# A hybrid attention and mLSTM decoder trunk in float32: the mLSTM's gates, running maximum and what goes with them placed at the end of attention instead of between its first units

## The chip, the cores and the metric

The kernel runs on one core of one Trainium2 chip. A core has a matrix engine (TensorE, here PE, with its weight loads as PEld), a vector engine (VectorE, DVE), a scalar engine (ScalarE, ACT), a general engine (GpSimd, POOL) and a queue engine (SyncE, SP) that issues DMAs. Each engine runs its own list of instructions in order and waits on semaphores for the others. Matrix products are written to PSUM, which is divided into banks of 128 x 512 float32.

The metric is the device time of one execution in microseconds, as the median of several runs.

## The reference

Two layers over 512 tokens of width 1024. Each layer computes, after an RMS norm:

```python
z = h @ w_in      # q_a | k_a | v_a | q_m | k_m | v_m | o_m | i/f gate logits | gates A, B
att = sliding_window_attention(q_a, k_a, v_a, sinks)        # 8 heads of 64, 2 kv heads, window 128
i_pre, f_pre = jnp.split(if_m + m_gate_bias, 2, axis=-1)
hm = mlstm_chunkwise(q_m, k_m, v_m, i_pre, f_pre)           # 4 heads, qk 64, v 128
mixed = sigmoid(g_a) * (att @ w_att_branch) + sigmoid(g_m) * (rmsnorm(hm) * sigmoid(o_m) @ w_m_branch)
x = x + mixed @ w_out
x = x + relu(rmsnorm(x) @ w_ff1)**2 @ w_ff2
```

The part that the change moves is the scalar side of the mLSTM: from the gate logits of 4 heads,

```python
log_f = log_sigmoid(f_pre);  b = cumsum(log_f)              # decay up to each token
m_t = max(b + m_prev, max over s <= t of (b_t - b_s + log_i_s))   # running maximum, the stabiliser
w   = exp(b_t - b_s + log_i_s - m_t) * (q_t . k_s)          # weights of the mLSTM
h   = (w @ v + ...) / max(|den|, exp(-m_t))
```

## The kernel before

All products keep float32 accuracy by splitting each operand into a high and a low part: a weight tile `w` of 128 x 512 is loaded by SP, ACT copies its rounded part to `wh` (L197) and DVE subtracts to get `wl` (L198). A projection is a group of four output banks (named mm in the profile) over eight chunks of 128 input rows; a chunk takes 4 x 3 = 12 matmuls of 512 columns.

In `mixer` a helper, `weave`, walks through a list of such steps, the fill, each of which counts 0.25, and calls side steps at given positions of that count (one unit is one chunk of 12 matmuls). After it a scheduler orders the instructions of each engine by what it expects to be ready, so an instruction does not stand exactly where the position says, but the positions set who comes first among what is ready. The fill here is: the mLSTM's q and k (positions 0 to 8), two groups of gate A (8 to 24), the mLSTM's v (24 to 32), the attention branch (32 to 40), a group of gate B (40 to 48), the o gate (48 to 56) and the last gate group.

The side steps are, in this order:

- Attention, in eight units: four blocks of 128 queries by two key/value heads. Of each unit: `att_scores` twice (product with kT, then ACT L567 or a memset and DVE's predicated copy L568 out of PSUM), `att_softmax` (maximum L575, L576, L578; four exponentials L581 and one L583; division L584 to L586), `att_probs` (four transposes, split by ACT L207 and DVE L208, masks on POOL L600 and L602), `att_out` (products with v2, then ACT L614, DVE L618, ACT L621, DVE L622). For each block, `k_tr` and `q_tr` transpose keys and queries (ACT L526, L527, L548; DVE L528, L529, L549). Unit i has its first score product at position 7 + 1.65 i and its `att_out` 5.65 later.
- `gating0`: i and f gates, log sigmoid (L405 to L417; twelve small operations on DVE and ACT).
- `gating1`: six small products with `lf` give sums along the tokens into an aux bank; DVE copies them to `bl` and `gr` (L426, L427), forms `acol` (L428) and the ten entries of `bias` (L431, L433).
- `gating2`: four transposes of `acol` into one aux bank, then four scans on DVE (L445), one a block, each started from the block before through `mp` (L448).
- `gating3`: the running maximum `cm` is split to `cm2` by ACT (L463) and DVE (L464), four small transposes of it and DVE's L468 and ACT's L470 give `em`.
- `qk_split` splits the mLSTM's q and k (L642 to L650).
- `m_decay` (product of `sel` with `cm2`, copied by ACT L710), `m_weights` (DVE L717, ACT L718 and L721, POOL L723, a product of k and q, DVE L729) and `m_out` (products with `vm`, then L737 to L742), for four heads from position 28 on.

All side steps share the PSUM pool aux, which has three banks here; a step's first product waits for a bank, which is free again when its last reader is done. ACT changes its function table between exponentials and the sigmoids of the gates (L655; `back` restores the table, L661).

Of the kernel before, what the change touches and what calls it, by code (L numbers as in the profile page):

```python
# [33 lines left out]
def hybrid_kernel(ctx, tc, x, norm_mix, w_in, att_q_norm, att_k_norm, att_sinks, m_gate_bias,  # L34
# [324 lines left out]
    def mixer(l, norm, late, order, phase):  # L359
# [154 lines left out]
        def k_vec(b):  # L514
            rope(kvi[:, b, 0:128].rearrange("p (h d) -> p h d", d=HD), b, HKV)

        def k_tr(b):

            ps = aux([P, P])
            pe.transpose(ps, kvi[:, b, 0:128], ident)  # L520
            for h in range(HKV):
                r = slice(64 * h, 64 * h + 64)
                o = slice(64 - 64 * h, 128 - 64 * h)
                c = slice((b + 1) * P, (b + 2) * P)
                g = gcols[1][r, l:l + 1]
                sc.activation(kTh[r, h, c], ps[r, :], AF.Copy, scale=g)  # L526
                sc.activation(kTh[o, h, c], ps[r, :], AF.Copy, scale=g)  # L527
                ve.scalar_tensor_tensor(kTl[r, h, c], ps[r, :], g, f32(kTh[r, h, c]), op0=ALU.mult, op1=ALU.subtract)  # L528
                ve.tensor_copy(kTl[o, h, c], f32(kTl[r, h, c]))  # L529

        def q_vec(b):
            rope(q_tok[b].rearrange("p (h d) -> p h d", d=HD), b, HQ)

        def q_tr(b):


            ps = aux()
            for j in range(4):
                pe.transpose(ps[:, j * P:(j + 1) * P], q_tok[b][:, j * P:(j + 1) * P], ident)
            for j in range(2):  # L540
                qT[b, j] = temp(F32R)
                t4 = qT[b, j].rearrange("p (n i t) -> p n i t", n=2, i=2)
                p4 = ps[:, 2 * j * P:2 * (j + 1) * P].rearrange("p (n t) -> p n t", n=2)
                for i in range(2):
                    r = slice(64 * i, 64 * i + 64)
                    o = slice(64 - 64 * i, 128 - 64 * i)
                    g = gcols[0][r, l:l + 1]
                    sc.activation(t4[r, :, i, :], p4[r], AF.Copy, scale=g)  # L548
                    ve.scalar_tensor_tensor(t4[o, :, i, :], p4[r], g, f32(t4[r, :, i, :]), op0=ALU.mult,  # L549
                                            op1=ALU.subtract)  # L550
# [87 lines left out]
        def qk_split(m, i):  # L638
            t = qk_raw[m]
            r, o = slice(64 * i, 64 * i + 64), slice(64 - 64 * i, 128 - 64 * i)  # L640
            d = slot(F32R)
            sc.activation(d[r], t[r], AF.Copy)  # L642
            if m < 2:
                gp.tensor_copy(d[o], f32(d[r]))
                low = slot(F32R)
                gp.memset(f32(low[o]), 0.0)
                ve.tensor_tensor(low[r], t[r], f32(d[r]), op=ALU.subtract)
                m_q[2 * m + i], m_ql[2 * m + i] = d, low
            else:
                ve.tensor_tensor(d[o], t[r], f32(d[r]), op=ALU.subtract)  # L650
                m_k[2 * (m - 2) + i] = d
# [24 lines left out]
        def ev_v(b, ps):  # L676
            if b == 0:
# [6 lines left out]
        side = [(0, lambda: k_vec(0)), (0, lambda: q_vec(0)), (0, lambda: k_vec(1)), (0, lambda: q_vec(1)),  # L684
                (7 - 1.25, lambda: k_tr(0)), (7 - 1.75, lambda: q_tr(0))]
        for i, (b, kv) in enumerate(units):
# [6 lines left out]
            if kv == 0 and b + 1 < NB:  # L693
                if b + 2 < NB:
                    side += [(at + 1, lambda b=b: k_vec(b + 2)), (at + 1, lambda b=b: q_vec(b + 2))]
                side += [(at + 2 * 1.65 - 1.25, lambda b=b: k_tr(b + 1)), (at + 2 * 1.65 - 1.75, lambda b=b: q_tr(b + 1))]
        side += [(8.45 + 3.0 * i, f) for i, f in enumerate((gating0, gating1, gating2, gating3))]
        side += [(9.6 + 1.65 * n, lambda n=n: qk_split(n // 2, n % 2)) for n in range(8)]
        g0, s0 = gate_steps(0)
        g1, s1 = gate_steps(1, lambda: back(sigmoid(g0 + g1)))  # L700
# [579 lines left out]
    for l in range(DEPTH):  # L1280
        with start if l == 0 else ExitStack() as phase:
            if l > 0:
                psum_pools(phase, 3)
            norm = mixer(l, norm, late, order, phase)
        late = norm.steps(1, 1.5, 0.5)
        with ExitStack() as phase:
            psum_pools(phase, 2)
            norm = mlp(l, norm, late, phase)
        late = norm.steps(0, 1.5, 0.5, lambda k, norm=norm: turn_behind(norm, k)) if norm else []
        order = [4, 5, 6, 7, 0, 1, 2, 3]  # L1290
# [40 lines left out]
```

## Time and profile before

| | us |
|---|---|
| median of 3 runs | 1310.16 |
| lowest and highest run | 1309.24, 1310.36 |
| the profiled execution | 1309.12 |
| its span | 1307.4 |
| TensorE busy in it | 1288.9 |
| VectorE, ScalarE, GpSimd busy | 954.2, 762.6, 219.3 |

The span goes from the first to the last instruction of the profiled execution. The granted clock was 1.00 throughout. In the views below, a row of the order of time gives start, length, engine, line, operation, output and inputs with sizes and a count; in brackets stands how long the engine was idle before and what ended that. A group's row gives busy us and the mean of one in ns.

The busy time of 40 slices, in tenths, shows the two layers, each with its attention and mLSTM first and its feed-forward part behind:

```profile
PE   8999999999999999999999999999999999999998
PEld 6877788888889999999888777888888899999986
DVE  4689754465677897968957896545737879879797
ACT  5468755444465665656554787554445556665563
POOL 4513300000003021131115223000000030301210
```

Counted from 1, attention of layer 0 is in slices 3 to 5 and that of layer 1 in slices 22 to 25 (32.7 us each): there VectorE is at its busiest outside the feed-forward part, and ScalarE at its busiest of all.

### The profile page before, as it was taken

To read this page: it belongs to the slowest core of one execution; us is meant where nothing else is said; L and a number is where in the kernel's file an instruction comes from. 1 tells how busy PE (TensorE), PEld (TensorE's weight loads), DVE (VectorE), ACT (ScalarE), POOL (GpSimd) and SP (SyncE) were. 2 spreads that over 40 slices of the span, in tenths; PEclk is the share of its full clock that TensorE was granted. 3 is DMA by queue.
4 is the path that set the end of the run, shared out by engine and by line. 5 is a ranking of instruction groups with operands and counts; after the bars stand their busy time and mean duration, and the time that the engine had idled before them with its cause. 6 is when DMAs were issued, how large, how long until landed. Compare 5 with 4: busy or idle time off the path is not lost.

```text
span 1307.4 us, 19100 instructions
## 1 busy us (share of the span) xinstructions
PE 1288.9 (99%) x6966; PEld 1103.1 (84%) x6966; DVE 954.2 (73%) x1501; ACT 762.6 (58%) x1327; POOL 219.3 (17%) x303
## 2 busy tenths in 40 slices
PE   8999999999999999999999999999999999999998
PEld 6877788888889999999888777888888899999986
DVE  4689754465677897968957896545737879879797
ACT  5468755444465665656554787554445556665563
POOL 4513300000003021131115223000000030301210
PEclk9999999999999999999999999999999999999999
DMA  5322222372369888897124222223714597988953
GB/s 154 110 73 65 65 76 78 89 243 87 97 154 171 237 185 206 197 209 213 33 70 117 65 65 73 76 79 90 256 56 129 143 214 193 204 212 196 213 144 95
DMA packets 129855, 177.62 MB, mean 136 GB/s; under 512 B 9816, under 2 KB 77504, under 8 KB 129760
## 3 DMA queue, kind: packets, MB, share of 16 engines
q1 hardware_dynamic: 93664, 131.69, 33.4%
q0 software_dynamic: 35520, 44.17, 21.2%
q8 instruction: 55, 0.90, 0.3%
q10 hardware_dynamic: 576, 0.53, 0.1%
q14 instruction: 40, 0.33, 0.1%
HBM read 174.27 MB, written 2.10 MB: 135 GB/s over the span
## 4 chain that ended last, share of the span: by engine, by line
PE 91%; DVE 4%; ACT 2%; issue 1%; POOL 1%; DMA 1%; DVEq 0%; ACTq 0%; POOLq 0%; SPq 0%
PE mm L47 74%; PE aux L47 15%; PE aux L52 2%; DVE wl L198 1%; ACT wh L197 1%; ACT t L581 0%; DMA w<-in_w_in_dram 0%; POOL t L602 0%; DVE t L618 0%; POOL t L476 0%; DVE t L208 0%; DMA grow<-in_norm_mix_dram 0%; DVE a L650 0%; DVE t L568 0%; DVE m L575 0%
## 5 line engine op out<-in xcount | busy, mean ns | idle before, releaser
L47 PE MATMUL mm<-i,wh 128*128 128x512 f32 (+1 forms) x1280 | 353.1, 362 | 0.3 <-ACT kvi L381 0.3
L836 ACT ACTIVATE wh<-raw 128x1024 fp32r<-128x1024 f32 x212 | 223.0, 1055 | 181.6 <-PE mm L47 110.7
L837 DVE TENSOR_TENSOR wl<-raw,wh 128x1024 fp32r<-128x1024 f32 x212 | 255.3, 1218 | 74.7 <-ACT wh L836 74.4
L47 PEld LDWEIGHTS mm<-i,wh 128*128 128x128 f32 x1280 | 223.8, 189 | 32.8 <-DVE a L668 0.9
L198 DVE TENSOR_TENSOR wl<-w,wh 128x512 fp32r<-128x512 f32 (+1 forms) x208 | 141.1, 682 | 131.3 <-ACT wh L197 122.7
L47 PE MATMUL mm<-i,wl 128*128 128x512 f32 (+1 forms) x640 | 230.4, 360 | 0.0
L197 ACT ACTIVATE wh<-w 128x512 fp32r<-128x512 f32 (+1 forms) x208 | 127.1, 612 | 139.9 <-PE mm L47 102.6
L47 PE MATMUL mm<-wh,uh 128*128 128x512 f32 x448 | 174.9, 390 | 0.0
L47 PE MATMUL mm<-wl,uh 128*128 128x512 f32 x448 | 174.8, 390 | 0.0
L47 PE MATMUL mm<-wh,ul 128*128 128x512 f32 x448 | 174.3, 389 | 0.0
L991 POOL DMA_DIRECT2D raw<-in_w_ff_dram x48 | 62.5, 1309 | 594.0 <-DVE i L211 284.3
L47 PE MATMUL mm<-wh,i 128*128 128x512 f32 (+1 forms) x512 | 150.0, 370 | 0.4 <-ACT wh L197 0.4
L47 PEld LDWEIGHTS mm<-i,wl 128*128 128x128 f32 x640 | 121.0, 189 | 18.4 <-DVE wl L837 0.4
L47 PEld LDWEIGHTS mm<-wh,i 128*128 128x128 f32 x512 | 92.1, 189 | 16.2 <-ACT wh L197 0.8
L879 DVE SCALAR_TENSOR_TENSOR x<-mm,ms,x 128x512 f32<-128x512 f32 x128 | 91.9, 744 | 12.2 <-PE mm L47 12.2
L47 PEld LDWEIGHTS mm<-wh,ul 128*128 128x128 f32 x448 | 84.1, 188 | 17.7
L47 PEld LDWEIGHTS mm<-wh,uh 128*128 128x128 f32 x448 | 84.3, 188 | 16.3
L47 PEld LDWEIGHTS mm<-wl,uh 128*128 128x128 f32 x448 | 84.3, 188 | 16.0
L47 PE MATMUL mm<-wl,i 128*128 128x512 f32 (+1 forms) x256 | 93.4, 365 | 0.0
L47 PE MATMUL mm<-wh,a 128*128 128x512 f32 x256 | 81.3, 393 | 0.0
L47 PE MATMUL mm<-a,wh 128*128 128x512 f32 x256 | 80.5, 397 | 0.0
L47 PE MATMUL aux<-t,wh 128*128 128x256 f32 x384 | 69.5, 283 | 0.0
(247 smaller groups left out, 2157.6 us busy)
## 6 DMA issues: line engine op xcount, KB each, us to landing
raw<-in_w_ff_dram SPq DMA_DIRECT2D x144, 512.0 KB, 5.2
raw<-in_w_ff_dram POOLq DMA_DIRECT2D x84, 512.0 KB, 7.9
w<-in_w_in_dram SPq DMA_DIRECT2D x128, 256.0 KB, 2.7
w<-in_w_out_dram SPq DMA_DIRECT2D x32, 256.0 KB, 2.9
w<-in_w_att_branch_dram SPq DMA_DIRECT2D x16, 256.0 KB, 2.7
w<-in_w_m_branch_dram SPq DMA_DIRECT2D x16, 256.0 KB, 2.8
w<-in_w_in_dram SPq DMA_DIRECT2D x16, 128.0 KB, 2.1
out_dram<-x SPq DMA_DIRECT2D x8, 256.0 KB, 2.0
```

The costliest lines, as they stand in the source:

```text
L47: latest[0] = nc.tensor.matmul(*args, **kw)
L52: return nc.tensor.transpose(*args)
L197: sc.activation(wh[:, :off], raw[:, :off], AF.Copy)
L198: ve.tensor_tensor(wl[:, :off], raw[:, :off], f32(wh[:, :off]), op=ALU.subtract)
L836: sc.activation(hi, src, AF.Copy)
L837: ve.tensor_tensor(lo, src, f32(hi), op=ALU.subtract)
L879: ve.scalar_tensor_tensor(xh, ps[:, i, :], ms[j][:, b:b + 1], xh, op0=ALU.mult, op1=ALU.add)
L991: gp.dma_start(to[h], src(h, i, j), accum_op=ALU.add)
```

## The change

One line of `mixer` gives the positions of the four gating steps. They were 8.45, 11.45, 14.45 and 17.45, between the score products of the first and the last units of attention; they become 20.5, 22.25, 24.0 and 25.75, around the probabilities and outputs of the last units and shortly before `m_decay` at 28. No operation is added, removed or resized.

```diff
-        side += [(8.45 + 3.0 * i, f) for i, f in enumerate((gating0, gating1, gating2, gating3))]
+        side += [(20.5 + 1.75 * i, f) for i, f in enumerate((gating0, gating1, gating2, gating3))]
```

The side steps that stand beside it in the code:

```python
units = [(b, kv) for b in range(NB) for kv in range(HKV)]
...
    at = 7 + 1.65 * i
...
side += [(9.6 + 1.65 * n, lambda n=n: qk_split(n // 2, n % 2)) for n in range(8)]
...
    at = 28 + 4.65 * h
    side.append((at, lambda h=h: m_decay(h)))
```

## The prediction

> **What bounds the kernel now.** I read the page first, then the busy time by stretch for the two attention stages, then what TensorE waited for there, then the order of time around those waits.
>
> ```profile
> PE 1288.9 (99%) x6966; PEld 1103.1 (84%) x6966; DVE 954.2 (73%) x1501; ACT 762.6 (58%) x1327; POOL 219.3 (17%) x303
> ...
> PE 91%; DVE 4%; ACT 2%; issue 1%; POOL 1%; DMA 1%; DVEq 0%; ACTq 0%; POOLq 0%; SPq 0%
> ```
>
> TensorE is busy 1288.9 of 1307.4 us and is 91% of the chain that ended last. The change takes no matmul away and adds none, so it can only alter TensorE's idle time. How much of that lies where the change acts is in the next view, with layer 0 in the first four rows and layer 1, 646.9 us later, in the last three.
>
> ```profile
> 62.00:104.40 42.40, 41.07 (x216) 32.68 (x215) 37.05 (x97) 30.45 (x89) 13.83 (x29) 1.00 0.26 69
> 104.40:150.00 45.60, 44.04 (x210) 34.24 (x209) 40.39 (x93) 38.52 (x96) 13.37 (x20) 1.00 0.25 67
> 150.00:161.50 11.50, 11.03 (x50) 8.54 (x50) 7.83 (x20) 7.65 (x22) 3.51 (x7) 1.00 0.21 61
> 161.50:200.00 38.50, 38.50 (x196) 32.70 (x195) 21.76 (x62) 21.96 (x62) 2.63 (x8) 1.00 0.30 82
> ...
> 708.90:751.30 42.40, 40.99 (x216) 32.63 (x215) 37.18 (x97) 30.34 (x89) 13.45 (x28) 1.00 0.26 69
> 751.30:796.90 45.60, 44.10 (x210) 34.21 (x209) 40.43 (x92) 38.53 (x96) 13.41 (x20) 1.00 0.25 67
> 796.90:808.40 11.50, 11.03 (x50) 8.54 (x50) 7.85 (x20) 7.66 (x22) 3.51 (x7) 1.00 0.19 59
> ```
>
> The columns are length, then the busy time of PE, PEld, DVE, ACT and POOL, the granted clock, and DMA. Attention of one layer shows 1.33 + 1.56 + 0.47 = 3.4 us of idle TensorE, and the mLSTM behind it none. DVE is busy 37.05 of 42.40 and 40.39 of 45.60 us (87% and 89%) in attention, ACT 72% and 84%; after it both fall under 60%. So attention is where VectorE and ScalarE sometimes make TensorE wait, and the change moves VectorE work out of it into its last few microseconds. Both layers show the same rows, so I work on layer 0 and double.
>
> ```profile
> PE aux L47 <- POOL t L602: 0.9, 2, 0.5
> PE aux L47 <- DVE t L568: 0.8, 1, 0.8
> PE aux L47 <- DVE kT L528: 0.5, 1, 0.5
> PE aux L52 <- DVE t L445: 0.3, 1, 0.3
> PE aux L47 <- DVE m L576: 0.2, 1, 0.2
> PE aux L52 <- DVE t L549: 0.2, 1, 0.2
> ```
>
> These are TensorE's named waits from 62 to 161.5 us: 2.9 us. One of them, 0.3 us for L445, is for the moved work itself: a PSUM bank of the pool aux (three banks) that the four scans of the running maximum hold from their transposes until the last scan. The largest, 0.8 us for L568, is in the first units, ahead of everything that moves, and stays.
>
> **What a wait costs.** The idle shown is less than the time lost, as the pace shows.
>
> ```profile
> 261.55 54.62 PE mm L47 x240
> ```
>
> ```profile
> 113.49 0.39 PE L47 MATMUL mm<-i,wl 128*128 128x512 f32 x1
> 114.15 0.33 PE L52 MATMUL aux<-ident,t 128*128 128x128 f32 x1 [0.28 <-DVE t L445]
> ...
> 123.30 0.61 PE L47 MATMUL mm<-i,wh 128*128 128x512 f32 x2
> 124.43 0.36 PE L47 MATMUL aux<-kT,t 128*128 128x256 f32 x1 [0.52 <-DVE kT L528]
> ...
> 152.26 0.39 PE L47 MATMUL mm<-wl,i 128*128 128x512 f32 x1
> 153.01 0.50 PE L47 MATMUL aux<-t,v 128*128 128x512 f32 x1 [0.36 <-POOL t L602]
> 153.35 0.39 PE L47 MATMUL aux<-cm,sel 128*128 128x512 f32 x1
> ```
>
> Undisturbed, one matmul of 512 columns starts every 54.62/240 = 0.23 us. From 113.49 to 114.15 are 0.66 us, so 0.43 is lost where 0.28 is shown; a wait costs its shown idle plus about 0.15. In this measure the wait for L528 costs 123.30 to 124.43 less two matmuls, 1.13 - 0.46 = 0.67; and 2.9 shown is about 2.9 + 8 x 0.15 = 4.1 us a layer.
>
> **The change, part by part.** gating0 does not move: its operations are ready early, and in the new order it stands on DVE and ACT where it stood. gating1, gating2 and gating3 do move, in both layers alike. SP's queue issues the same loads in the same order, and POOL's queue changes one place; no DMA is added. ACT keeps its four table loads in attention at the same steps. In the new program order on TensorE gating1's six products stand right behind the transposes of the last attention unit's probabilities, the transposes of acol half a chunk of projection later, and the four small transposes of the running maximum one by one among the next chunk and a half; then comes the first product with sel, 2.25 chunks behind gating1. From the second weight product of the mLSTM on, both orders are equal.
>
> The moved instructions and their neighbours, from the groups by line and shape of 62 to 160 us:
>
> ```profile
> L618 DVE TENSOR_TENSOR t<-aux,t 64x256 f32<-64x256 f32 x16 | 6.6, 414 | 1.8 <-ACT t L614 1.5
> ...
> L622 DVE TENSOR_TENSOR a<-t,a 128x128 fp32r<-128x128 f32 x16 | 4.4, 297 | 0.4 <-ACT a L621 0.4
> ...
> L445 DVE TENSOR_TENSOR_SCAN t<-aux,mp,neg 4x128 f32<-4x128 f32 x4 | 1.9, 466 | 0.0
> ...
> L464 DVE TENSOR_TENSOR cm<-t,cm 4x512 fp32r<-4x512 f32 x1 | 0.7, 681 | 0.0
> ...
> L463 ACT ACTIVATE cm<-t 4x512 fp32r<-4x512 f32 x1 | 0.6, 633 | 0.0
> ...
> L448 DVE TENSOR_TENSOR mp<-t,gr 4x1 f32<-4x1 f32 x3 | 0.4, 142 | 0.0
> ...
> L426 DVE COPY bl<-aux 128x32 f32<-128x32 f32 x1 | 0.2, 179 | 0.0
> L428 DVE TENSOR_TENSOR acol<-ig,bl 128x16 f32<-128x16 f32 x1 | 0.2, 175 | 0.0
> ```
>
> ```profile
> 84.45 0.18 DVE L426 COPY bl<-aux 128x32 f32<-128x32 f32 x1
> ...
> 85.66 0.69 DVE L586 TENSOR_TENSOR t<-t,den 128x512 f32<-128x512 f32 x1
> 86.27 0.16 DVE L431 COPY bias<-acol 128x4 f32<-128x4 f32 x1
> ```
>
> *What attention gets back.* gating1's thirteen DVE operations ran from 84.45 to 86.43; with the softmax's L586 of 0.69 us between them taken off, they are some 1.2 us of DVE (busy times of neighbours overlap). The four scans are 1.9, the three L448 0.4, L464 0.7. So 4.2 us a layer leave DVE's queue in attention, 5% of its 77 us there, and one PSUM bank is free from acol's transposes to the last scan.
> - The wait for L445 goes: -0.43. Bounds: 0 (another holder of a bank takes its place) to -0.43.
> - The wait at 124.43 is for the last unit's keys. In the new order ACT runs all four L526/L527 for them without the L614 that stood between, so the second L528 comes sooner; I take -0.45, between 0 and -0.67.
> - The wait for L576 (0.2 shown, 0.35 lost) goes, but the probabilities of the fifth unit and the scores of the last now come in one cluster with it and need three banks at once: +0.2 net, between -0.35 and +0.6.
> - Of the two waits for L602 (0.9 shown, 1.2 lost), the later, 0.5, falls away because gating1 and acol now stand between the last probabilities and the products that need their masks; of the earlier I take 0.2 off. -0.7, between 0 and -1.2.
> - TensorE's own 1.1 us of gating leaves the early units and comes back at the end. TensorE then comes sooner to the keys of the third block and the second scores of the fifth unit, which wait for DVE: I take nothing as won or lost, bounds -0.3 (acol's own wait) and +0.5.
>
> Sum: -0.43 - 0.45 + 0.2 - 0.7 = -1.4 us a layer.
>
> *What the end of attention pays.* Here the whole chain gating1, gating2, gating3 has to be over before sel. DVE runs in order, and in the new order between L426 and L464 stand four L618, four L622, one weight split and em's sum: 4 x 0.41 + 4 x 0.25 + 0.7 + 0.2 = 3.5 us, beside 1.2 + 1.9 + 0.4 + 0.7 = 4.2 of the chain itself. With ACT's 0.6 for L463 and about 0.8 for the crossings to TensorE and back, sel is ready 9.1 us after gating1's products. TensorE's cover up to sel is 2.25 x 12 x 0.23 = 6.2 us of projection, 8 x 0.23 = 1.8 of attention output, and some 0.65 for the transposes of acol and of the running maximum: 8.7 us. Missing: 0.4 us a layer. Bounds: 0, since the L618 run while TensorE transposes acol, and 3.4 when the masks hold DVE up (second rival). Behind the waiting sel stand the first weight products and the projection's matmuls, and nothing else is in a hurry:
>
> ```profile
> 156.45 0.60 ACT L710 ACTIVATE t<-aux 128x512 f32<-128x512 f32 x1
> ```
>
> ```profile
> 167.11 0.38 PE L47 MATMUL aux<-vm,t 128*128 128x129 f32 x2
> ```
>
> The copy of sel's product, L710, ran 3 us after sel (153.35), and the first product that needs the weights made of it came 10.7 us after that. The weight splits that DVE delays by 0.6 us are made up to three chunks (8 us) ahead.
>
> Net: -1.4 + 0.4 = -1.0 us a layer, -2.0 us in all. The profiled execution took 1309.12 us (span 1307.40 and 1.72 around it); -2.0 makes 1307.1. The median of the runs shown lies 1.04 above the profiled one, so the forecast for it is 1308.2 us.
>
> **The rivals.** *The end is covered and attention flows better.* If nothing is missing before sel and the freed DVE time also removes the fifth unit's cluster wait and the rest of L528 and L602, a layer gains 0.43 + 0.67 + 0.35 + 0.9 = 2.35: 1310.16 - 4.7 = 1305.5. For it speaks that DVE is at 89%; against it that the first units' waits do not depend on what moves.
>
> *Slower: the masks hold the chain.* The moved sums with two SBUF inputs (L428, L433, L448) now fall beside POOL's masks of the last unit.
>
> ```profile
> 100.77 0.56 DVE L578 TENSOR_TENSOR es<-sinks,m 128x4 f32<-128x4 f32 x1
> ```
>
> ```profile
> 99.59 1.73 POOL L644 CAST a<-a 64x512 fp32r<-64x512 f32 x1 [25.72 <-ACT a L642]
> ```
>
> ```profile
> L602 POOL TENSOR_SCALAR_AFFINE_SELECT t<-t 128x512 fp32r<-128x512 f32 x12 | 9.5, 788 | 4.8 <-DVE es L578 2.5 <-DVE t L208 1.9
> ...
> L600 POOL TENSOR_SCALAR_AFFINE_SELECT t<-t 128x512 fp32r<-128x512 f32 x12 | 8.5, 712 | 20.4 <-ACT t L207 20.4
> ```
>
> L578, of four elements a partition, took 0.56 us and ended with POOL's cast at 101.3. The last unit has two L600 and two L602, 2 x 0.71 + 2 x 0.79 = 3.0 us. If DVE stands through all of them, sel misses 0.4 + 3.0 = 3.4 us a layer, and the layer loses 3.4 - 1.4 = 2.0: 1310.16 + 4.0 = 1314.2. It decides from 1.4 us missing on. Against it: L650 and L622, also with two SBUF inputs, ran at their usual length beside masks. The Trainium skill, SBUF — State Buffer, section Who interferes with whom, says that a DVE instruction with two SBUF inputs contends with a GpSimd instruction that reads SBUF and the second fully blocks. The row of L578 agrees; by the rule alone each such sum would wait for a mask's end, which is this rival's 1314.2.
>
> *Nothing is won.* The scheduler reorders some 400 matmuls, and each wait removed is followed by one like it at the next bank: 1310.2. For it speaks that the first score waits stay and that TensorE, arriving sooner, meets the same VectorE.
>
> **How the numbers follow.** Forecast 0.42, covered end 0.20, slower 0.25, nothing won 0.13. A measurement of this kernel can tell about 0.2%, 2.6 us, from no change. The forecast's 2.0 us gain is close to that: of its 0.42 I give 0.22 to faster, 0.19 to within, 0.01 to slower. So faster 0.22 + 0.20 = 0.42, within 0.19 + 0.13 = 0.32, slower 0.25 + 0.01 = 0.26. The forecast's own range, from its terms' bounds with not all at one end, is -2.2 to +0.3 us a layer: 1305.8 to 1310.8. The range for 8 in 10 reaches on to both rivals: 1303.5 to 1315.0.
>
> **What would show it.** Right: no wait of PE for L445 inside attention; TensorE's idle in the stretch that holds units three to seven falls below 1.56 us; a wait of 0.2 to 0.8 us in front of aux<-cm,sel or of the small transposes, released by L464 or L445. The covered end: no such wait at all. The masks: L428 and L433 of 0.5 us and more beside L600 and L602, and a wait over 1.4 us before sel. Nothing won: the same 3.4 us of idle a layer under other names. The forecast is wrong in its ground if the mLSTM behind, without idle now, shows waits for L729 or L680.

## The result, and the profile after

The changed kernel took 1311.70 us (median of 22 runs, 1310.85 to 1313.08) and the kernel before, on the same chip, 1310.26 (22 runs, 1308.73 to 1311.04). The ratio is 1.0014, with a 95% interval of 1.0008 to 1.0020: slower by 0.14%, 1.4 us by the medians and 1.8 by the ratio. That is less than the 0.2% that the prediction took as the least a measurement of this kernel can tell, but the interval doesn't reach 1, and the time has moved to the other side of the 2 us gain that was forecast. The profiled execution took 1311.39 us, its span is 1309.7.

TensorE's busy time on the page of the changed kernel is 1288.8 us (98%), what it was (1288.9 before), so the 2.3 us of span are idle or slower starts on TensorE. To place them I use three marks that both kernels have on TensorE: A, the transposes of the first block's queries; B, the transposes of the last unit's probabilities; C, the second weight product of the mLSTM, behind which both orders are equal. From A to C the same 309 matmuls of the projections stand in both kernels, 276 of them ahead of B. The place of A itself differs from profile to profile (61.03 and 61.44 here, 62.79 in the last run below, an edit of the kernel before that changes nothing up to there), so I compare distances between the marks and not spans. The rows of the order of time of the kernel before:

```profile
61.03 0.27 PE L52 MATMUL aux<-ident,a 128*128 128x128 f32 x1
...
149.97 0.40 PE L52 MATMUL aux<-ident,t 128*128 128x128 f32 x2
...
161.49 0.33 PE L47 MATMUL aux<-a,a 128*128 128x384 f32 x1
```

and of the changed kernel:

```profile
61.44 0.38 PE L52 MATMUL aux<-ident,a 128*128 128x128 f32 x2
...
149.16 0.30 PE L52 MATMUL aux<-ident,t 128*128 128x128 f32 x1 [0.17 <-ACT wh L197]
...
162.91 0.33 PE L47 MATMUL aux<-a,a 128*128 128x384 f32 x1
```

A to B went from 88.94 to 87.72 us, 1.2 less, since the TensorE work of gating1 to gating3 no longer stands there; B to C went from 11.52 to 13.75, 2.2 more. A layer pays 1.0 us. Layer 1 gives the same to 0.1 us (A to B 88.99 and 87.70, B to C 11.52 and 13.74).

What TensorE waited for, from 62 to 162.9 us (total, times, longest), in the changed kernel:

```profile
PE aux L52 <- DVE t L568: 1.3, 2, 0.8
PE aux L47 <- DVE t L568: 0.9, 1, 0.9
PE aux L47 <- DVE t L618: 0.8, 1, 0.8
PE aux L47 <- DVE kT L528: 0.7, 1, 0.7
PE aux L52 <- ACT a L621: 0.3, 1, 0.3
...
```

Beside the same view of before: the waits for L445, L576 and L549 are gone, and that for L602 (0.9) has left the list. New are 0.8 and 0.5 for L568 in front of the keys of the third and fourth block, and 0.8 for L618 in front of the first scores of the sixth unit; the 0.3 put down to L621 stand in front of the first small transpose, where the first scan had ended only 0.15 us before. The wait for L528, of which the forecast hoped to be rid, grew from 0.5 to 0.7. Why a removed delay came back as a wait is seen at the third block's keys. TensorE before:

```profile
93.25 0.61 PE L47 MATMUL mm<-i,wh 128*128 128x512 f32 x2
94.05 0.30 PE L52 MATMUL aux<-ident,kvi 128*128 128x128 f32 x1 [0.18 <-DVE t L549]
```

TensorE after:

```profile
92.58 0.39 PE L47 MATMUL mm<-i,wh 128*128 128x512 f32 x1
93.75 0.30 PE L52 MATMUL aux<-ident,kvi 128*128 128x128 f32 x1 [0.78 <-DVE t L568]
```

VectorE after:

```profile
91.04 0.69 DVE L198 TENSOR_TENSOR wl<-w,wh 128x512 fp32r<-128x512 f32 x1 [1.32 <-ACT wh L197]
...
93.17 0.44 DVE L568 COPY_PREDICATED t<-tri_l,aux 128x256 f32<-128x256 int32 x1
```

Counted from A, the keys' transpose starts 33.02 us behind it before and 32.31 after, so 0.7 is won. But TensorE was ready for it 1.3 us sooner (0.18 and 0.78 of idle time are to be taken off these starts); the other 0.6 became a longer wait. VectorE had stood idle for 1.32 us shortly before, waiting for ScalarE, so it wasn't short of time here: L568 came when its turn in the order came.

At the wait for L528 it was another thing. The second L528 of the last block started at 123.90, 0.44 sooner than before when counted from A, as the forecast had it, but TensorE was there 0.58 sooner. ScalarE's copy for it was over at 123.11, in the kernel before at 123.32 with L528 at 123.93: in both kernels VectorE came last, and the L614 that the forecast saw leave ScalarE's way was not what held it. Between the two L528 of the changed kernel stand L650 with 0.92 us and L529 with 0.65, which took 0.69 and 0.22 elsewhere.

At the end stands what the forecast had no price for. TensorE in the changed kernel, around the third and fourth of gating3's small transposes:

```profile
157.81 0.40 PE L47 MATMUL mm<-wh,i 128*128 128x512 f32 x1
158.14 0.22 PE L52 MATMUL aux<-ident,t 4*128 4x4 f32 x1
158.29 0.50 PE L47 MATMUL mm<-wh,i 128*128 128x512 f32 x1
158.63 0.39 PE L47 MATMUL mm<-wl,i 128*128 128x512 f32 x1
...
159.42 0.22 PE L52 MATMUL aux<-ident,t 4*128 4x4 f32 x1
...
160.84 0.40 PE L47 MATMUL aux<-cm,sel 128*128 128x512 f32 x1
```

From 157.81 to 158.63 stand two projection matmuls, 0.46 us at the undisturbed pace of 0.23, and one transpose of four columns: 0.82, so the transpose costs 0.36 us with no wait shown on PE. It starts 0.10 late, the matmul behind it 0.15 later, and the one behind that again 0.11 late. The product with sel, which the forecast saw waiting, starts right after its forerunner with no wait in brackets.

### The profile page after: what moved, and what is told of

The parts are those of the page before. It is cut to its first block, busy times and chain, and to the rows that moved or that the text cites. A ratio compares the mean times of both kernels' runs of the same rounds, so it can differ in the third digit from the quotient of the medians.

```text
span 1309.7 us, 19099 instructions
## 1 busy us (share of the span) xinstructions
PE 1288.8 (98%) x6966; PEld 1104.8 (84%) x6966; DVE 957.2 (73%) x1501; ACT 761.4 (58%) x1327; POOL 215.0 (16%) x303
## 4 chain that ended last, share of the span: by engine, by line
PE 93%; DVE 4%; ACT 1%; issue 1%; POOL 0%; DMA 0%; DVEq 0%; ACTq 0%; POOLq 0%
PE mm L47 76%; PE aux L47 14%; PE aux L52 2%; DVE wl L198 1%; ACT wh L197 1%; DVE t L618 0%; DVE t L208 0%; DVE t L549 0%; ACT t L581 0%; DVE a L650 0%; DMA grow<-in_norm_mix_dram 0%; DVE t L568 0%; DVE kT L528 0%; POOL t L602 0%; DVE kT L529 0%
## 5 line engine op out<-in xcount | busy, mean ns | idle before, releaser
L47 PE MATMUL aux<-i,wh 128*128 128x256 f32 x384 | 69.5, 283 | 0.0
```

Source lines behind the costliest of these rows:

```text
L47: latest[0] = nc.tensor.matmul(*args, **kw)
```

## Experiments

The theory with which I went in (A) was that the end got dearer because each of the four small transposes stands alone. Its rivals were that VectorE's chain is late there (B), and that the loss lies in the new waits of attention (C). All ratios are against runs of the kernel before on the same chip; line numbers of an edited kernel are shifted by the lines added (L570 or L577 for L568, for instance).

**The four together, in the changed kernel.**

```diff
-            for b in range(NB):
-                pe.transpose(cps[:, b * MH:(b + 1) * MH], cm[:, b * P:(b + 1) * P], ident[:MH, :MH])
+            last = pe.transpose(cps[:, 3 * MH:], cm[:, 3 * P:], ident[:MH, :MH])
+            with tc.issue_after(last.ins):
+                for b in range(NB - 1):
+                    pe.transpose(cps[:, b * MH:(b + 1) * MH], cm[:, b * P:(b + 1) * P], ident[:MH, :MH])
```

> The changed kernel, but the last gating step's four transposes of the running maximum to columns (128x4) stand together on TensorE instead of one by one between projection products; nothing else moves. Theory A (the end of attention got dearer because each of the four stands alone and costs about 0.36 us instead of 0.08): 0.7 to 1.0 us less in each layer, so 1.4 to 2.0 us under the changed kernel, about 1310 us. Theory B (the end got dearer because VectorE's chain of gating is late there, and TensorE waits for it): within 0.5 us of the changed kernel, the wait only moves from the first transpose to the group. Theory C (the loss is not at the end but in the new waits for aux banks between the units): within 0.3 us of the changed kernel.

Measured: 1310.09 us, ratio 1.0002 (0.9993 to 1.0011), level with the kernel before. A to B is 87.67 us as in the changed kernel, B to C 12.96 in place of 13.75. TensorE there:

```profile
157.75 0.61 PE L47 MATMUL mm<-wh,i 128*128 128x512 f32 x2
158.87 0.38 PE L52 MATMUL aux<-ident,t 4*128 4x4 f32 x4 [0.51 <-DVE t L445]
...
159.52 0.63 PE L47 MATMUL mm<-wh,i 128*128 128x512 f32 x2
```

The group has to wait for the last scan, 0.51 us, which the four apart did not, and is cheaper all the same: 1.77 us from 157.75 to 159.52 less three matmuls (two ahead of the group, one behind it), 0.69, is 1.08 with the wait, against 1.77 for the four apart (0.69, the first of them with a wait of 0.31, then 0.36, 0.36 and 0.35). As A expected (1.6 us under the changed kernel); B's lateness exists, with 0.5 us, but is not what made the kernel slower.

**One by one and together, in the kernel before.** A function `small_tr(b)` issues one transpose behind the latest matmul, `gating4` the rest of gating3:

```diff
+        side += [(29.0 + 0.75 * b, lambda b=b: small_tr(b)) for b in range(NB)] + [(31.4, gating4)]
```

> The kernel before, with the same four transposes put one by one, 0.75 of a projection group apart, behind the last unit's output products; the rest of the gating stays early between the units. Their data are ready tens of microseconds before. Theory A: against its twin with the four together at the same place, 0.8 to 1.0 us more in each layer, 1.6 to 2.0 us in all. Theories B and C: within 0.4 us of the twin, since nobody waits for data and the units are the same in both.

The twin has `29.0 + 0.0 * b` and 29.2 for gating4; TensorE's orders differ in nothing but these four.

> The twin: the kernel before, with the four transposes together behind the last unit's output products. Theory A: within 0.5 us of the kernel before (four for 0.34 us at either place). Theories B and C say nothing else of it; if it is over 1 us slower, moving them alone costs something that none of the three has.

Measured: 1313.23 us one by one, ratio 1.0026 (1.0015 to 1.0036), and 1311.60 together, 1.0013 (1.0004 to 1.0021). The twins are 1.6 us apart, at the lower end of what A said, with the data ready long before and every other instruction of TensorE in the same order: standing apart costs that by itself. One of the four by itself:

```profile
161.71 0.39 PE L47 MATMUL mm<-wh,i 128*128 128x512 f32 x1
162.03 0.22 PE L52 MATMUL aux<-ident,t 4*128 4x4 f32 x1
162.18 0.50 PE L47 MATMUL mm<-wh,i 128*128 128x512 f32 x1
162.52 0.40 PE L47 MATMUL mm<-wl,i 128*128 128x512 f32 x1
```

0.81 less 0.46 is 0.35 us; the twin's four together:

```profile
156.77 0.40 PE L47 MATMUL mm<-wh,i 128*128 128x512 f32 x1
157.09 0.41 PE L52 MATMUL aux<-ident,t 4*128 4x4 f32 x4
157.43 0.50 PE L47 MATMUL mm<-wh,i 128*128 128x512 f32 x1
157.77 0.40 PE L47 MATMUL mm<-wl,i 128*128 128x512 f32 x1
```

1.00 less 0.46 is 0.54 for all four. In the kernel before they cost the same 0.54: there they follow four large transposes, and the second matmul behind starts at 126.19, 1.21 us after the first transpose (124.98); behind acol's four transposes, with no small ones, it is 0.67 (99.81 to 100.48). The expectation had 0.34. The twin missed the rest of it too: it is 1.95 us over the kernel before, not within 0.5. Its A to B is 89.54 us, 0.6 more than before although the four have left that stretch. Of that, 0.23 is one projection matmul that stands ahead of B here (277 and not 276) and is missing behind it; for the rest, other waits came: 0.6 us for L627 and 0.4 for L587, neither of them among the waits of the kernel before (L618 and L578 there).

**Only the last gating step late.**

```diff
-        side += [(8.45 + 3.0 * i, f) for i, f in enumerate((gating0, gating1, gating2, gating3))]
+        side += [(8.45 + 3.0 * i, f) for i, f in enumerate((gating0, gating1, gating2))] + [(25.75, gating3)]
```

> The kernel before, with only the last of the four gating steps moved to the place that the change gives it; the cumulative sums, the biases and the running maximum stay early. Its four transposes then go together. Theory A: within 0.5 us of the kernel before, so 1 to 2 us under the changed kernel. Theory B: the same, since the chain before it is early. Theory C: within 0.5 us of the kernel before where the new waits between the units come from the first three steps' absence; as slow as the changed kernel where they come from the fourth's.

Measured: 1310.28 us, ratio 1.0004 (0.9995 to 1.0013), 0.6 over the kernel before and not told apart from it. A to B is 89.35, 0.4 more than before, B to C 11.18, 0.3 less; here too one projection matmul of 0.23 us has changed from behind B to ahead of it, so the two together say more: 0.1 more. Position 25.75 for gating3 is not the trouble as long as its four transposes go together, as they do here with the running maximum long complete.

**Gating1 to gating3 left out** (gating0 stays).

```diff
-        side += [(20.5 + 1.75 * i, f) for i, f in enumerate((gating0, gating1, gating2, gating3))]
+        side += [(20.5 + 1.75 * i, f) for i, f in enumerate((gating0, nothing))]
```

> The changed kernel with the cumulative sums, the biases, the running maximum and its transposes left out (the biases stay 0, the floor of the denominators 1, the running maximum 0, so the output is not the reference's): the last unit's end without what the change puts there. Theory A: TensorE's lost time up to the last unit's transposes stays at the 8.2 us of both kernels, since waits there only change place; all that is saved is saved at the end: 1.1 us of TensorE's own gating work and 1.0 to 1.3 us of lost time in each layer, 4.2 to 4.8 us under the changed kernel, about 1307. The prediction's step (the gating in the middle costs 1.4 us of waits in each layer, which its absence gives back): the lost time up to there is 6.7.

Measured: 1306.60 us, ratio 0.9977 (0.9968 to 0.9986), by the ratios 4.8 us under the changed kernel, as A expected. Its marks:

```profile
62.12 0.38 PE L52 MATMUL aux<-ident,a 128*128 128x128 f32 x2
...
149.74 0.30 PE L52 MATMUL aux<-ident,t 128*128 128x128 f32 x1 [0.17 <-ACT wh L197]
...
160.89 0.33 PE L47 MATMUL aux<-a,a 128*128 128x384 f32 x1
```

and its waits from 62 to 162.9 us:

```profile
PE aux L52 <- DVE t L572: 1.3, 2, 0.8
PE aux L47 <- DVE t L572: 0.9, 1, 0.9
PE aux L47 <- DVE t L622: 0.7, 1, 0.7
PE aux L47 <- DVE kT L532: 0.7, 1, 0.7
```

This run sets the prices. A to B is 87.62 us, the changed kernel's 87.72: the four largest rows of the changed kernel's waits stand here too, with nothing of the moved work anywhere, so they are attention's own once the gating has left its middle, and no consequence of where it went. B to C is 11.15. The gating of one layer therefore costs (88.94 - 87.62) + (11.52 - 11.15) = 1.3 + 0.4 = 1.7 us at its early place, and 0.1 + (13.75 - 11.15) = 2.7 us at the late one. Two layers of the difference are 2.0 us; the medians gave 1.4, the ratio 1.8 and the spans 2.3, of which 0.4 lie ahead of A. Theory C falls as the cause of what the end lost: these waits stay in the run with the four together, which is level with the kernel before. But they have a part.

At the early place 1.3 us from A to B is less than TensorE's own time for the moved work there. Read from starts as above, gating1's products cost 0.83 (83.19 to 84.71 less three matmuls), acol's transposes 0.44 (99.81 to 100.48 less one) and the small ones 0.54, together 1.8. So with the work gone, some 0.5 us of it comes back as such waits.

**All four steps ahead of the first unit**, positions `1.0 + 1.75 * i`, the small transposes together.

> The kernel before with the four gating steps all ahead of the first unit (positions 1, 2.75, 4.5 and 6.25), where TensorE had no wait in either kernel, and the four small transposes together. Theory A: lost time up to the last unit's transposes 8.1 to 8.3 us as in both kernels, at the end about 0.7 as where only the last step is late or less, none added ahead of the first unit: 0.3 to 0.5 us a layer under the kernel before, about 1309. The prediction's step: the middle without gating loses 6.7 us, 1.4 less in each layer, about 1306.5. If the gating holds up the normalization ahead of the units: slower than before by over 1 us.

Measured: 1315.37 us, ratio 1.0044 (1.0032 to 1.0057). All the gains expected were missed. A to C is 102.1 us with most of the gating ahead of A; the largest wait behind it is for L570, 2.1 us in two, one of them 1.6. These copies of the scores (L568 in the kernel before, where the wait is 0.8) keep TensorE longer in the first units. Which shift of the order does that was not tried.

**Between the last four units**, positions `16.0 + 1.75 * i`, the small transposes together.

> The four gating steps between the last four units (positions 16, 17.75, 19.5 and 21.25), the four small transposes together: a place between that of before and that of the change. Theory A: within 0.8 us of the kernel before, as at the other two places once the transposes stand together. The prediction's step: the waits of the middle stay won, 1 us or more under the kernel before.

Measured: 1312.89 us, ratio 1.0023 (1.0014 to 1.0032). Both expectations missed: standing together isn't enough. The four waits of the run without gating remain, and the small transposes add one of their own, 0.6 us for L445.

**The four together behind the first weight products, in the changed kernel**, with `small_tr` at 31.0.

> The changed kernel with the four small transposes together behind the first weight products, so that nothing on TensorE waits for the running maximum but the selection product. Theory A: as fast as with the four together ahead of the selection product, within 0.7 us, or up to 0.7 us faster (the 0.5 us wait for the last scan becomes a wait of 0.2 to 0.5 us at the selection product): 1309.3 to 1310.1. Theory B (lateness of VectorE's chain decides): the selection product waits 0.8 us or more and nothing is gained against the changed kernel beyond 0.5 us.

Measured: 1310.94 us, ratio 1.0011 (1.0002 to 1.0020), above A's range by 0.8, and between the changed kernel (1.0014) and the four together in front of sel (1.0002) with intervals that overlap both. In its trace the four have moved past C, B to C is 12.63, and the wait has moved as foreseen:

```profile
159.29 0.61 PE L47 MATMUL mm<-wh,i 128*128 128x512 f32 x2
160.39 0.47 PE L47 MATMUL aux<-cm,sel 128*128 128x512 f32 x1 [0.49 <-DVE cm L464]
```

With the four together, the gating's chain is some 0.5 us too long for its cover, whether the first reader waits for the last scan (0.51 in front of sel) or for L464 (0.49 here). On time the run decides nothing.

**The same numbers by products in fp32r.** The running maximum lies in cm2 as two halves in fp32r, the rounded type of the split operands, and the first column of sel adds them, so each transpose can be written as

```diff
-                pe.transpose(cps[:, b * MH:(b + 1) * MH], cm[:, b * P:(b + 1) * P], ident[:MH, :MH])
+                pe.matmul(cps[:, b * MH:(b + 1) * MH], cm2[:, b * P:(b + 1) * P], sel[:, :, 0], start=True, stop=True)
```

It went into the run with the four one by one, into the changed kernel, and into the kernel before.

> As the run with the four small transposes one by one behind the last unit, but each of the four is a product of cm2 (both halves of the running maximum) with the first column of sel, of the same result, with both inputs fp32r as in the projection around it, instead of a transpose in fp32. If the 0.355 us of each come from the change of type from fp32r to fp32 and back: each costs 0.06 to 0.12 us, and the run is 1.9 to 2.4 us under the one with fp32 transposes one by one, about 1311. If they come from standing alone (a load of other weights for four columns): each stays at 0.3 us or more, and the time within 0.5 us of that run, about 1313.

> The changed kernel with the four transposes as such products in fp32r; the order then puts them together right in front of the selection product, since they need cm2. Theory A: the isolated switches go (1.2 to 1.5 us of loss become one wait of 0.4 to 0.8 us for L464), so 0.6 to 1.0 us less in each layer than the changed kernel: 1309.6 to 1310.5, level with the kernel before. Theory B (lateness): the wait in front of them is 1 us or more and the time within 0.5 us of the changed kernel.

> The kernel before with the same four products instead of the transposes, at their old place. There the four stand together behind other fp32 transposes, so little is to be won: within 0.5 us of the kernel before, at best 0.3 us a layer faster.

Measured: one by one 1311.14 us, ratio 1.0010 (1.0001 to 1.0019), in place of 1.0026 in fp32; in the changed kernel 1310.48, 1.0007 (0.9998 to 1.0016); in the kernel before 1310.39, 1.0004 (0.9996 to 1.0013). One product alone:

```profile
161.50 0.40 PE L47 MATMUL mm<-wh,i 128*128 128x512 f32 x1
161.73 0.17 PE L47 MATMUL aux<-sel,cm 128*128 128x4 f32 x1
161.76 0.48 PE L47 MATMUL mm<-wh,i 128*128 128x512 f32 x1
162.08 0.40 PE L47 MATMUL mm<-wl,i 128*128 128x512 f32 x1
```

0.58 less 0.46 is 0.12 us, against 0.35 for the transpose, and the start is no longer late. The time came out as expected for a change of type. But the product also has 128 rows of weights where the transpose has 4, and the traces speak against the type. Each kernel has other fp32 transposes that stand alone between fp32r matmuls, those of the keys of the first two blocks, with 128 rows; in the changed kernel:

```profile
74.63 0.39 PE L47 MATMUL mm<-i,wl 128*128 128x512 f32 x1
74.86 0.27 PE L52 MATMUL aux<-ident,kvi 128*128 128x128 f32 x1
74.89 0.71 PE L47 MATMUL mm<-i,wh 128*128 128x512 f32 x2
75.44 0.40 PE L47 MATMUL mm<-i,wl 128*128 128x512 f32 x1
```

From 74.63 to 75.44 are 0.81 us with three matmuls, 0.69: this fp32 transpose costs 0.12, as the fp32r product does. The weight loads show the difference, first the keys', then that of the small transpose at 158.14 (4*128 are the rows and columns of its weights):

```profile
74.63 0.14 PEld L52 LDWEIGHTS aux<-ident,kvi 128*128 128x128 f32 x1
...
158.14 0.13 PEld L52 LDWEIGHTS aux<-ident,t 4*128 4x128 f32 x1 [0.36 <-DVE t L618]
```

The first runs beside the matmul in front, which started at 74.63 too. The second starts 0.33 after the matmul in front of it (157.81), with the transpose itself. The idle 0.36 put down to L618 is not a wait for data: in the run with the four one by one, where the data are ready long before, a small transpose starts just as late (161.71 to 162.03). A third lone fp32 transpose, of 24 rows, at 29.99 in the changed kernel, costs 0.37 (29.67 to 30.50 less two matmuls). So the dear ones are those with weights of few rows between matmuls with 128, whose load isn't hidden; fp32 alone does not do it. An fp32r product with 4 rows, which would show whether fp32 has any part, was not run.

The run with the products one by one came in as expected, and so did the changed kernel with them: the order puts its four together, in front of sel, behind a wait of 0.50 for L464, so B's wait of 1 us didn't appear. In the kernel before they are 0.6 over its median, just outside the 0.5 expected and not told apart from it.

No version is faster than the kernel before. The run without gating is 2.9 us under it, and that is about the most that any better place in this order could win, the gating's own matmuls included.

## Why the prediction was wrong

- *What bounds the kernel* held: nothing behind the first weight products changed.
- *What attention gets back, -1.4 a layer.* This step failed first. The waits for L445 and L576 went and those for L602 nearly did, as said. But "TensorE's own 1.1 us of gating leaves the early units and comes back at the end ... I take nothing as won or lost, bounds -0.3 and +0.5" was where it came back: the keys of the third block and the sixth unit's first scores wait 0.78 each, and the wait for L528 grew to 0.7 where 0.45 was to be won, since VectorE and not L614 on ScalarE held it. TensorE's own work there was 1.8 us, not 1.1, and A to B shortened by only 1.2; taking the work out altogether shortens it by 1.3. So nothing was won beyond the work that left, and 0.6 of that was lost to new waits. That is the rival "nothing is won", given 0.13, for its stretch; its 1310.2 then lacked the dearer end. My ground for more, VectorE at 87 to 89%, was an average: at the third block's keys it had been idle for 1.32 us shortly before, while at the sixth unit's first scores and at L528 it had been busy, but with work that does not move.
- *The waits for L602, -0.7.* This term was right, about: the later one, 0.36 shown, and one of 0.10 behind it are gone from B to C, where they made the next starts 0.52 and 0.27 late (152.26 to 153.01 less one matmul, 153.58 to 154.31 less two), and the earlier one shrank from 0.51 to 0.08.
- *What the end of attention pays, +0.4.* This step failed most: wrong term and wrong size. I counted "some 0.65 for the transposes of acol and of the running maximum" as cover, time in which VectorE can work. It was cover, and sel waits for nothing. But it was also TensorE's time at the end of the layer, and the four alone took 1.77 us of it, 1.23 more than the 0.54 that they cost in their group in the kernel before; 0.31 of this is the wait in front of the first, the rest is standing apart. The chain itself took 10.9 us (149.63 to the end of L464 at 160.56) where 9.1 was forecast; sel did not wait because the small transposes' own loss made the cover 11.2 (to 160.84) where 8.7 was forecast. With the four together the wait came, 0.5 for the last scan, so the absence of the forecast wait is no proof of a short chain. The order one by one was read correctly beforehand; what was not asked is what a step costs by itself, which only the start-to-start times of neighbours show.
- *Slower: the masks hold the chain.* The place was right, the weight was not. One of VectorE's sums, L428, fell beside the second of the last unit's four masks on POOL (L602, 151.28 to 152.05), which stand back to back from 150.49 to 153.36:

```profile
151.68 0.39 DVE L428 TENSOR_TENSOR acol<-ig,bl 128x16 f32<-128x16 f32 x1
```

  L428 took 0.39 us where it took 0.175 before, and ended at 152.07, 0.02 behind this mask; gating1's thirteen operations took 2.3 us (151.47 to 153.74) instead of 1.2. The Trainium skill, SBUF — State Buffer, section Who interferes with whom, lets the second of two such instructions stand until the first is over, and L428 agrees. But this rival decides only from 1.4 us missing in front of sel on, and no wait stands there in the trace.
- *The sum.* Forecast a layer: -0.9 in the stretch from A to B, -0.5 for the later wait for L602, +0.4 for the end, -1.0. Measured: +0.6 from A to B (1.8 of work left, 1.2 was won), -0.8 for the waits for L602 behind B, and +1.2 for the four transposes beyond their 0.54 in a group: +1.0. The rest of the gating costs about as much behind B (some 1.3) as it did ahead of it.

## What to carry to other kernels

Price a step that moves by what it costs in its new company, not by its row in the old: the same four transposes cost 0.54 us together and 1.4 apart. In this kernel, where the engine that bounds it works through a fixed order, a delay removed ahead of a wait was mostly paid again at the next wait; leave the work out in one run, as here, and see what its place costs before hoping for more. A place that looks untidy may be the cheapest: none of the other placements tried beat the early one. And a run that meets its expected time does not yet prove the reason behind the expectation: the fp32r products came in on time, and the rows of the keys' transposes, which were in every trace, speak for another reason.

## What the runs showed of the hardware

An fp32 transpose of 4 rows and 4 columns, alone between fp32r matmuls of 128 rows and 512 columns, cost 0.35 to 0.36 us in each of six places read in two kernels (a further one of a group 0.06), with no idle time in brackets on PE; its weight load started 0.33 us behind the matmul in front. One of 24 rows cost 0.37. An fp32 transpose of 128 rows in such a place cost 0.12, and so did the fp32r product with 128 rows that replaces the small one; the keys' load started together with the matmul in front. PE's waits can't show such a loss: it has to be read from the starts of the neighbours, and its cause from the rows of PEld.
